# Transposing x out of DRAM instead of SBUF in a convolution kernel that runs on TensorE

## The chip, the cores and the metric

The kernel runs on one core of a Trainium2 chip. The metric is the device time in microseconds of one execution. The profile of one execution stands beside it; its span, from the first to the last instruction, is a little shorter than the time.

## The reference

A causal convolution over the sequence with eight taps, each tap a full 512 x 512 matrix:

```python
B, S, D, K = 8, 4096, 512, 8
out = np.zeros_like(x)                       # x: [B, S, D] float32
for k in range(K):                           # kernel: [K, D, D] float32
    shifted = x if k == 0 else np.concatenate(
        [np.zeros((B, k, D), np.float32), x[:, :-k, :]], axis=1)
    out += np.matmul(shifted, kernel[k])
```

## The kernel before

The 32768 rows of x are cut into 128 runs of 256 rows, one run for each partition. A step of the loop takes the next K = 8 rows of every run; there are NIT = 32 steps. TensorE needs x with its feature dimension on the partitions, so every step transposes its 8 x 128 rows of x, in two halves of four (h = 0, the low half, and h = 1, the high half), into the tile XT.

The way of x in the kernel before: GpSimd issues a DMA that reads 1 MB of f32 and writes it, cast to bf16, into an SBUF tile `xin` of 128 x 2048. SyncE then issues a DMA transpose from `xin` to a half of XT. The pool holds two `xin` buffers, so the load of a half waits until the transpose of the half two before it has read its buffer.

```python
xpool = ctx.enter_context(tc.tile_pool(name="x", bufs=2))
XT = spool.tile([P, K, D], bf, name="XT")
...
def load(out, src):
    nc.gpsimd.dma_start(out=out, in_=src)            # line 80 of the kernel

xin = {}

def load_x(i, h):
    xin[i, h] = xpool.tile([P, 4, D], bf, name="xin")
    load(xin[i, h], xr[:, K * i + 4 * h:K * i + 4 * h + 4, :])

def transpose_x(i, h):                               # line 89
    nc.sync.dma_start_transpose(
        out=XT[:, 4 * h:4 * h + 4, :].rearrange("p j (c m) -> p (j c) m", m=P),
        in_=xin[i, h].rearrange("p j d -> p (j d)"))
```

The eight taps are not multiplied one by one. The kernel uses a nested scheme of sums and differences (three levels, each of which needs three products in place of four), so VectorE forms sums of rows of XT (D1, D2, D4, D21, D42 and so on) and sums of results in PSUM. In a step there are three nodes, MID, LO and HI, with nine products of four matmuls each. The sums that read a freshly transposed half first are:

```python
def prep_m():                                        # reads XT[0:2], of the low half
    tt(D1[:, 0:2], XT[:, 7::-7], XT[:, 0:2], ADD)
    tt(pairs(D2[:, 1:5]), pairs(XT)[:, 3::-3], pairs(XT)[:, 0:2], ADD)

def prep_d4(h):
    a, b = (XT[:, 4:8], XT[:, 0:4]) if h == LO else (XT[:, 0:4], XT[:, 4:8])
    tt(D4[:, 4 * h:4 * h + 4], a, b, ADD)            # h == HI needs the new high half
```

The steady loop, one pass for each node. All engines run their own instructions in the order in which they are written here:

```python
for k, (i, a) in enumerate(order):                   # a: MID, LO, HI for each step i
    ...
    if a == MID and more:
        transpose_x(i + 1, 0)
    node_l(cur, 0, LO)
    node_l(cur, 0, HI)
    if nxt:
        node_a0(nxt)
        node_u(nxt)
    node_l(cur, 1, LO)
    node_e(cur, 0)                                   # result out of PSUM, or stored
    if nxt:
        node_seed(nxt, 0)
        node_seed(nxt, 1)
        node_dts(nxt)
    if a == MID:
        prep_d421(LO)
        prep_d41(HI)
    elif a == LO:
        if more:
            prep_m()
        prep_d421(HI)
    elif more:
        prep_d41(LO)
        prep_d42(LO)
        prep_d21()
    if nxt:
        for b_ in range(2):
            node_v(nxt, b_)
            node_d(nxt, b_)                          # VectorE: dts and v to the seed of node_l
    if a == MID:
        prep_d42(HI)
        prep_d27()
    elif more:
        prep_d4(LO if a == LO else HI)
    node_l(cur, 1, HI)
    if k + 2 < len(order):
        node_a1(k + 2)
    node_e(cur, 1)
    if a == LO and more:
        transpose_x(i + 1, 1)
        if i + 2 < NIT:
            load_x(i + 2, 0)
            load_x(i + 2, 1)
```

Steps 0 and 1 stand ahead of the loop in an order of their own, in which the loads and transposes appear so (all other work cut):

```python
load_x(0, 0); load_w(4); ...; load_x(0, 1); load_x(1, 0); ...; load_w(1); load_x(1, 1)
load_x(2, 0); load_x(2, 1); mid_acc(HI, LO)          # an accumulating DMA on a weight, SBUF to SBUF
transpose_x(1, 1); ...; transpose_x(2, 0); ...; load_x(3, 0); ...
load_x(3, 1); ...; transpose_x(2, 1); ...
```

The halves (0, 0), (0, 1) and (1, 0) are transposed on TensorE at the start; the other 61 are DMA transposes.

Of the kernel before, what the change touches and what calls it, by code (L numbers as in the profile page):

```python
# [22 lines left out]
def kernel(  # L23
# [7 lines left out]
    B, S, D = x.shape  # L31
    K = kernel.shape[0]
    P = 128
# [5 lines left out]
    bf = mybir.dt.bfloat16  # L39
# [12 lines left out]
    xpool = ctx.enter_context(tc.tile_pool(name="x", bufs=2))  # L52
# [26 lines left out]
    def load(out, src):  # L79
        nc.gpsimd.dma_start(out=out, in_=src)  # L80

    xin = {}

    def load_x(i, h):
        xin[i, h] = xpool.tile([P, 4, D], bf, name="xin")
        load(xin[i, h], xr[:, K * i + 4 * h:K * i + 4 * h + 4, :])

    def transpose_x(i, h):
# [52 lines left out]
    H, HF = XT, D421.bitcast(f32).rearrange("p (t b) d -> p t (b d)", b=2)  # L141
    nc.sync.dma_start(out=HF, in_=xr[:, RUN - 4:RUN, :])
    load_x(0, 0)
    zero = spool.tile([P, D], bf, name="zero")
    nc.vector.memset(zero, 0.0)  # L145
# [218 lines left out]
    transpose_pe("he", 1, H, 1, 4)  # L364
    load_w(7)
    load_x(0, 1)
    nc.vector.tensor_copy(out=XF[:, 6:8], in_=bank["xb"])
    tt(D2, XF[:, 1:6], XF[:, 3:8], ADD)
    fill(pair(2))
    tt(D4[:, 2:4], XF[:, 2:4], XF[:, 6:8], ADD)  # L370
    load_x(1, 0)
    direct(0, 2)
    tt(to(E4[:, 1:4]), prev(bank["he"]), to(XF[:, 1:4]), ADD)
# [278 lines left out]
```

## Time and profile before

| | |
|---|---|
| time, median of 2 runs | 779.34 us (779.1 to 779.57) |
| span of the profiled execution | 777.3 us |
| TensorE (PE) busy | 766.8 us, 99% |
| VectorE (DVE) busy | 657.5 us, 85% |
| ScalarE (ACT) busy | 284.9 us, 37% |
| granted TensorE clock | 1.000 |
| HBM read, written | 77.33 MB, 67.11 MB |
| DMA transposes | 61, median 6.1 us from issue to landing |
| loads of x | 64, median 5.9 us from issue to landing |

Busy time says how long an engine had something running; a matmul is pipelined, so a busy TensorE need not be one at its peak. In the lines of a timeline the columns are: start in us, duration in us, engine, line of the kernel, operation, output <- input by the program's names, their shapes, how many instructions are merged (x1), and in brackets the idle time of the engine ahead of it with what ended it. PE is TensorE, SPq the instruction queue of SyncE, POOL GpSimd. A transpose's or store's duration on SPq is the time for which it holds SyncE's queue, not the time until its data has landed. The queue lines of the page give packets, megabytes and the time that the packets took as a share of sixteen DMA engines over the span.

### The profile page before, as it was taken

Reading aid. Unit: us, or ns where it says so; the run is one execution under the profiler, and the core shown is the slowest. Engines: PE = TensorE matmul, PEld = TensorE weight load, DVE = VectorE, ACT = ScalarE, POOL = GpSimd, SP = SyncE. Lnnn points to the kernel's source line nnn. Section 1 sums busy time; section 2 is a strip of 40 time slices with the busy share of each in tenths; the row PEclk is TensorE's granted clock in tenths of the full one; section 3 lists DMA queues with packets and bytes.
Section 4 is the critical chain, followed back from the end, with each engine's and each line's share of the span. In section 5 each row is a group of like instructions: output and inputs, shape, how many; then the busy total and the mean of one; then the engine's idle time right before and its main releaser. Section 6 shows DMA issues by size and latency. Waiting matters only on the chain.

```text
span 777.3 us, 9450 instructions
## 1 busy us (share of the span) xinstructions
PE 766.8 (99%) x3584; PEld 347.3 (45%) x3584; DVE 657.5 (85%) x766; ACT 284.9 (37%) x462; POOL 42.3 (5%) x80
## 2 busy tenths in 40 slices
PE   7999999999999999999999999999999999999997
PEld 3444444444444444444444444444444444444443
DVE  4999988898888898888898888898888898888895
ACT  3553343333343333343333343333343333343332
POOL 4000000000000000000000000000000000000000
PEclk9999999999999999999999999999999999999999
DMA  9986878868786877787877878877697867687843
GB/s 199 211 125 170 226 185 178 208 159 190 164 199 163 197 172 189 164 198 169 194 171 187 164 174 190 207 162 188 163 187 176 207 158 190 165 186 179 204 133 121
DMA packets 159373, 139.42 MB, mean 179 GB/s; under 512 B 130144, under 2 KB 134240, under 8 KB 159200
## 3 DMA queue, kind: packets, MB, share of 16 engines
q1 hardware_dynamic: 145456, 99.89, 46.1%
q0 software_dynamic: 13728, 38.67, 31.6%
q8 instruction: 28, 0.46, 0.2%
q10 hardware_dynamic: 144, 0.26, 0.1%
q14 instruction: 17, 0.14, 0.1%
HBM read 77.33 MB, written 67.11 MB: 186 GB/s over the span
## 4 chain that ended last, share of the span: by engine, by line
PE 96%; DMA 2%; POOL 1%; ACT 0%; issue 0%; DVE 0%; DVEq 0%; POOLq 0%
PE pp L197 96%; DMA xin<-in_x_dram 2%; POOL w L80 0%; PE pp L186 0%; ACT y L295 0%; DVE y L76 0%; DVE pp L76 0%; POOL xin L80 0%; DVEq L647 0%; ACT pp L256 0%; ACT pp L244 0%; POOL XT L80 0%; PE pp L180 0%; POOL ident masks.py:199 0%; POOL ident masks.py:197 0%
## 5 line engine op out<-in xcount | busy, mean ns | idle before, releaser
L197 PE MATMUL pp<-w,D 128*128 128x512 bf16 x3280 | 715.5, 379 | 1.3 <-DVE w L76 0.9
L197 PEld LDWEIGHTS <-D 128*128 128x128 bf16 x3280 | 320.4, 98 | 389.8 <-issue 2.8
L76 DVE TENSOR_TENSOR D<-D 128x1024 bf16<-128x1024 bf16 (+1 forms) x252 | 228.2, 945 | 1.6 <-ACT D L353 1.6
L76 DVE TENSOR_TENSOR y<-pp,ms 128x1024 f32<-128x1024 f32 (+1 forms) x121 | 146.5, 1212 | 45.5 <-PE pp L197 45.4
L76 DVE TENSOR_TENSOR D<-XT 128x2048 bf16<-128x2048 bf16 (+2 forms) x153 | 142.1, 946 | 8.5 <-DMA XT<-xin 6.7
L244 ACT COPY pp<-pp 128x512 f32<-128x512 f32 x95 | 54.1, 570 | 256.0 <-PE pp L197 256.0
L256 ACT COPY pp<-pp 128x512 f32<-128x512 f32 x95 | 54.1, 570 | 170.6 <-PE pp L197 167.6
L76 DVE TENSOR_TENSOR pp<-dts,pp 128x512 f32<-128x512 f32 x95 | 65.5, 690 | 46.2 <-ACT dts L262 44.6
L299 ACT COPY ms<-pp 128x1024 f32<-128x1024 f32 x60 | 61.0, 1016 | 33.1 <-PE pp L197 33.1
L80 POOL DMA_DIRECT2D xin<-in_x_dram x64 | 34.2, 535 | 688.3 <-DMA XT<-xin 670.6
L272 DVE SCALAR_TENSOR_TENSOR pp<-pp,dts 128x512 f32<-128x512 f32 x95 | 65.9, 693 | 3.2
L262 ACT COPY dts<-pp 128x512 f32<-128x512 f32 x95 | 57.4, 604 | 2.0 <-PE pp L197 2.0
L258 ACT ACTIVATE pp<-pp 128x512 f32<-128x512 f32 x95 | 56.0, 589 | 1.2 <-DVE y L76 1.2
L197 PE MATMUL pp<-w,XT 128*128 128x512 bf16 x120 | 30.8, 379 | 0.0
L76 DVE TENSOR_TENSOR w<-w,w 128x2048 bf16<-128x2048 bf16 x18 | 21.6, 1219 | 0.4 <-DMA w<-in_kernel_dram 0.2
L197 PEld LDWEIGHTS <-XT 128*128 128x128 bf16 x120 | 11.7, 98 | 14.2
L180 PE MATMUL pp<-zero 128*128 128x512 bf16 x24 | 8.9, 505 | 2.4 <-DVE zero L145 1.2
L197 PE MATMUL pp<-w,w 128*128 128x512 bf16 x36 | 9.0, 379 | 1.3 <-ACT pp L244 0.7
L197 PE MATMUL pp<-w,F 128*128 128x512 bf16 x36 | 8.9, 379 | 0.0
L338 DVE MEMSET D<- 128x64 bf16 x2 | 0.2, 112 | 8.2 <-ACT D L351 7.7
L80 POOL DMA_DIRECT2D w<-in_kernel_dram x8 | 6.0, 766 | 0.8 <-DMA w<-in_kernel_dram 0.8
L197 PEld LDWEIGHTS <-w 128*128 128x128 bf16 x36 | 3.5, 97 | 5.8 <-issue 2.1
(55 smaller groups left out, 70.6 us busy)
## 6 DMA issues: line engine op xcount, KB each, us to landing
out_dram<-y SPq DMA_DIRECT2D x123, 512.0 KB, 3.5
xin<-in_x_dram POOLq DMA_DIRECT2D x64, 512.0 KB, 5.9
w<-in_kernel_dram POOLq DMA_DIRECT2D x8, 512.0 KB, 15.9
D<-in_x_dram SPq DMA_DIRECT2D x1, 1024.0 KB, 4.9
out_dram<-ms SPq DMA_DIRECT2D x2, 512.0 KB, 4.2
out_dram<-f SPq DMA_DIRECT2D x2, 512.0 KB, 3.7
XT<-xin SPq DMA_TRANSPOSE x61, 6.1
w<-w POOLq DMA_DIRECT2D x1, 512.0 KB, 9.9
```

The source lines that it names most:

```text
L76: nc.vector.tensor_tensor(out=o, in0=a, in1=b, op=op)
L80: nc.gpsimd.dma_start(out=out, in_=src)
L180: nc.tensor.matmul(pw[:, h], lhsT=zero[:, 0:P], rhs=zero, start=True, stop=True)
L197: nc.tensor.matmul(bank, lhsT=comp[:, c * P:(c + 1) * P], rhs=w[:, c, :], start=start and c == 0, stop=c == DC - 1, skip_group_check=True)
L244: nc.scalar.copy(out=n.q[:, 0], in_=n.q[:, 1])
L256: nc.scalar.copy(out=n.p[b_][:, 1], in_=n.q[:, 1])
L258: nc.scalar.mul(out=n.p[b_][:, 1], in_=n.q[:, 1], mul=-1.0)
L262: nc.scalar.copy(out=n.dts, in_=n.q[:, 0])
L272: nc.vector.scalar_tensor_tensor(out=p[:, 0], in0=p[:, 1], scalar=-1.0, in1=n.dts, op0=MUL, op1=SUB)
L299: nc.scalar.copy(out=ms[b_], in_=p)
L338: nc.vector.memset(z[:, :, 0:D:G], 0.0)
```

## The change

From the fourth step on (i = 3, counted from 0) the cast load of x writes into one of six DRAM buffers instead of one of two SBUF buffers, and the DMA transpose reads its source there. Steps 0 to 2 keep the SBUF tiles. What is computed stays the same, and so do the order of the instructions on each engine and the destination of the transposes. The aim is to take the staging copy of x out of SBUF and to give the loads more buffers to run ahead into.

```diff
@@ -81,8 +81,11 @@
 
     xin = {}
 
+    dpool = ctx.enter_context(tc.tile_pool(name="xd", bufs=6, space=bass.MemoryType.DRAM))
+
     def load_x(i, h):
-        xin[i, h] = xpool.tile([P, 4, D], bf, name="xin")
+        pool = xpool if i < 3 else dpool
+        xin[i, h] = pool.tile([P, 4, D], bf, name="xin" if i < 3 else "xd")
         load(xin[i, h], xr[:, K * i + 4 * h:K * i + 4 * h + 4, :])
 
     def transpose_x(i, h):
```

## The prediction

> **What bounds the kernel now.** I read the page's chain of work that ended last first, then the merged instructions of one steady period, then what one pair of transposes took to land, then the DMA queues. The chain, in order of time, ends so:
>
> ```profile
> 45.87 726.95 PE pp L197 x3364
> 772.82 0.02 issue
> 772.85 0.69 DVE y L76
> ```
>
> From 45.87 us on TensorE never waits. 726.95 us / 3364 matmuls = 216.1 ns each, and the starts of nearly all matmuls in the trace are 215 or 216 ns apart, whatever the DMAs do beside them. Nothing that the change touches lies on this stretch, so it can only leave it alone or put waits into it. Before 45.87 us the change alters nothing, as the first affected load comes later. That leaves next to nothing to win.
>
> The stretch holds 3364 / 108 = 31 periods (a step of the loop is three nodes of nine products of four matmuls: 108 x 216.1 ns = 23.3 us). Each period needs one transpose for each half of x. The merged timeline of one period, the lines that matter:
>
> ```profile
> 171.48 0.53 POOL L80 DMA_DIRECT2D xin<-in_x_dram  x1 [12.18 <-DMA XT<-xin]
> 173.93 4.82 SPq L89 DMA_TRANSPOSE XT<-xin  x1
> 176.90 0.69 DVE L76 TENSOR_TENSOR pp<-dts,pp 128x512 f32<-128x512 f32 x1 [1.69 <-ACT dts L262]
> 179.49 0.57 ACT L244 COPY pp<-pp 128x512 f32<-128x512 f32 x1 [2.80 <-PE pp L197]
> 182.30 1.82 DVE L76 TENSOR_TENSOR D<-XT 128x1024 bf16<-128x1024 bf16 x2
> 185.17 0.69 DVE L76 TENSOR_TENSOR pp<-dts,pp 128x512 f32<-128x512 f32 x1
> 187.27 0.57 ACT L244 COPY pp<-pp 128x512 f32<-128x512 f32 x1 [2.75 <-PE pp L197]
> 189.21 3.24 SPq L89 DMA_TRANSPOSE XT<-xin  x1
> 194.27 1.23 DVE L76 TENSOR_TENSOR D<-XT 128x2048 bf16<-128x2048 bf16 x1
> 194.71 0.53 POOL L80 DMA_DIRECT2D xin<-in_x_dram  x1 [13.19 <-DMA XT<-xin]
> ```
>
> The low half is issued at 173.93 and first read at 182.30 (prep_m); the high half is issued at 189.21 and first read at 194.27 (prep_d4). Landing of these two, low half first, as the trace gives it for the transpose line in windows around each:
>
> ```profile
> DMA to landing us min/median/max: 6.5/6.5/6.5
> ```
>
> ```profile
> DMA to landing us min/median/max: 5.0/5.0/5.0
> ```
>
> So the low half lands at 180.4, 1.9 us ahead of its reader, and the high half at 194.2, only 0.1 us ahead. What VectorE does after a late read decides whether TensorE feels it. TensorE needs node_d's first half at the start of the next node, which I take from the copy that follows node_a1, the last product of a node: 179.4, 187.2. In the MID node that node_d ended at 176.90 + 0.69 = 177.6 after an idle 1.69 us, so between the high half's read and TensorE there are 0.1 + 1.7 + 1.8 = 3.6 us of room. In the LO node it ended at 185.9, so the low half has 1.9 + 1.3 = 3.2 us. **The transposes may land at about issue + 8.6 (high) and issue + 9.7 (low) before TensorE waits.**
>
> The page's queues give the other limit:
>
> ```profile
> q1 hardware_dynamic: 145456, 99.89, 46.1%
> q0 software_dynamic: 13728, 38.67, 31.6%
> ```
>
> Together 78% of sixteen DMA engines: 0.78 x 23.3 = 18.1 us of each period, and 5.2 us free.
>
> **What the Trainium skill says.** The Trainium skill, page "DMA: Bandwidth & Descriptors", section "Latency and other measured facts", gives a transpose 261 GB/s with a non-contiguous middle dimension: 524 KB then take an estimated 2.0 us on the engines. The trace is a little slower, with SBUF as source: the packet records of the high half run from issue + 1.91 to + 4.51 us, 2.6 us or 202 GB/s.
> The same page of the Trainium skill, section "Why small descriptors are slow (HBM only)", puts the penalty on small pieces of HBM and exempts SBUF to SBUF. That is the risk here: a transpose has 2048 packets of 256 bytes. No run so far shows such pieces read from HBM.
> The same page of the Trainium skill, section "Queues, rings and completion order", says that an engine takes turns between queues at packet granularity. The trace agrees badly: beside the load issued at 171.48, the store issued at 173.43 and the transpose begin their packets only at about 176 and 177.2, when the load's are done. A short transfer waits for loads already queued.
>
> **The change part by part.** It removes no instruction of TensorE, VectorE or ScalarE, and no load and no transpose. It moves 58 of the 61 transposes and 58 of the 64 loads (29 of 32 steps, two halves) to DRAM buffers.
>
> Loads: each still reads 1 MB of f32. Its packets (8 KB read, 4 KB written, per engine 8) take 322 ns in the median, about the 25 GB/s at which the source is read; a store's 4 KB packet into DRAM takes 159. The read side still sets the pace, so I add nothing. A later receipt from DRAM costs nothing: six buffers instead of two put a load three steps ahead of its use.
>
> Traffic: 58 x 0.524 = 30.4 MB more written to HBM and as much read, 144 to 205 MB, 264 GB/s over the span. That alone is no reason to wait.
>
> Transposes: the cost that decides. From SBUF a packet takes 22.7 ns in the mean; 128 packets per engine are 2.9 us. For HBM as source I draw a line through the two kinds of cast loads: 2048 bytes read in 98 ns (weights), 8192 in 322 (x). Slope 224 / 6144 = 0.0365 ns per byte, intercept 23.3 ns. At 256 bytes: 23.3 + 9.3 = 33 ns, 128 x 33 = 4.2 us, against the 2.6 measured: each transpose lands 1.6 us later, at about issue + 6.6 and + 8.1. Both are inside the room. DMA occupancy rises by 2 x (4.2 - 2.9) = 2.6 us to 20.7 of 23.3 us, 89%. In the steady state the sum is 0 us on the path. VectorE will idle before prep_d4 more often, and catch up.
>
> Start: with two buffers, the load of step 3 waited for the transpose of step 2 (it issued at 58.09 us). With six free DRAM buffers GpSimd has nothing to wait for, and issues all six loads of steps 3, 4 and 5 right after the accumulate at 44.94, from 45.8 to about 49 us. Each is 8 x 0.4 = 3.3 us of all engines, so some 20 us of queue. The transpose of step 2's low half issues at 46.19, lands at 57.5 now and is read at 61.46, 4 us of room plus about 2 to TensorE. If it shares evenly with the burst it ends some 3 us later: no loss. If it queues behind the loads already issued (two or three), 7 to 10 us later: 1 to 4 us lost once. I put +1.5 us.
>
> Sum: 779.3 + 0 + 1.5 = 780.8 us.
>
> **The rivals.**
> First, the read from HBM is slow enough to become the bound. At 48 ns per packet a transpose takes 6.1 us and the high half's room is used up; at about 43 ns (5.5 us) the engines' 5.2 free us per period are gone. At 60 ns, 7.7 us each, a period holds 12.3 + 15.4 = 27.7 us of DMA, and the 29 affected periods cost 29 x 4.4 = 128 us. For it: the small pieces, latency under load, and a kernel whose high half has 0.1 us to spare already. Against it: the estimate has a third in hand, and the skill's transpose figure is fast. One case in four.
> Second, the burst is worse than I think, and store and transpose queue behind all six loads: the low half of step 2 lands near 74, 12 us late, TensorE loses 6 to 10 us, about 1%.
> Third, the transposes get faster: SBUF no longer carries source and load, and SyncE is held for less than the 3.2 to 4.8 us of now. But a transpose that lands early helps nobody: TensorE waits for nothing. It would end between 777 and 780 us.
>
> **The range and the chances.** Below is closed by the fixed pitch of 216 ns: 2% off would be 15.6 us, more than all TensorE idles in the whole run (777.3 - 766.8 = 10.5). So faster gets 0.01. The likely case lies from 778 to 784; the worse burst reaches 790; slow HBM reads, with a weight of 0.24, run from 800 far upwards. An interval for 8 in 10 is 777.5 to 810; 781 as the point.
>
> **What would show it.** Right: the chain again one piece of TensorE of about 727 us; transposes from DRAM landing 6 to 8.5 us after issue, 256-byte packets at 25 to 40 ns; DMA share near 0.85 to 0.9; a knot of six loads at 46 us and a landing of step 2's low half after 58 us. Wrong: VectorE's idle before reads of XT (now 6.7 us, six times in the whole run) growing past 100 us, with TensorE waiting for node_d in every period; that would mean packets over 45 ns. A transpose that lands sooner than from SBUF would refute the straight line, though not the time.

## The result, and the profile after

| | before | after |
|---|---|---|
| time, median of 2 runs | 779.34 us | 900.64 us |
| span of the profiled execution | 777.3 us | 898.7 us |
| TensorE busy | 766.8 us, 99% | 771.2 us, 86% |
| mean granted TensorE clock | 1.000 | 0.935 |
| HBM written | 67.11 MB | 97.52 MB |
| loads of x to landing, median | 5.9 us | 21.2 us (those into DRAM) |
| DMA transposes to landing, median | 6.1 us | 5.4 us (from DRAM), most 60.2 us |

The ratio is 1.156, 95% interval 1.152 to 1.159: 121 us slower, far outside the predicted range of 777.5 to 810.

The page of the changed kernel, with the span in 40 slices (22.5 us each; digits are tenths busy, PEclk tenths of the full TensorE clock):

```profile
PE   7980813106999999999999999999999999999997
...
PEclk9995865656999999999999999999999999999999
DMA  9999999999554444444455544454545444445553
```

All of the loss lies in slices 3 to 10. After some 217 us TensorE is as busy as before, and the DMA engines are *less* busy than before (0.49 in the windows from 216.7 to 869.7 us, where the kernel before has 0.73 to 0.81): work that belongs there has been done earlier. The instructions of GpSimd at the start of that stretch show which:

```profile
44.53 0.53 POOL L80 DMA_DIRECT2D xin<-in_x_dram  x1 [15.74 <-DMA XT<-xin]
45.06 0.90 POOL L172 DMA_DIRECT2D w<-w  x1
45.62 3.47 POOL L80 DMA_DIRECT2D xd<-in_x_dram  x6
52.08 0.52 POOL L80 DMA_DIRECT2D xd<-in_x_dram  x1 [2.99 <-DMA xin<-in_x_dram]
54.70 0.52 POOL L80 DMA_DIRECT2D xd<-in_x_dram  x1 [2.10 <-DMA w<-w]
57.40 0.52 POOL L80 DMA_DIRECT2D xd<-in_x_dram  x1 [2.18 <-DMA xd<-in_x_dram]
```

The six loads go out, as expected, but then a seventh follows, and an eighth, each when an earlier *load or accumulate* has landed, eight DMAs back (the built program gives GpSimd's DMAs eight semaphores in turn). None waits for a transpose to free a buffer. The last of the 58 loads is issued at 197.9 us and the last load packet ends at 217.7 us. GpSimd's waits over the whole run (us in total, times, longest) say the same, first in the kernel before, then in the changed one:

```profile
POOL xin L80 <- DMA XT<-xin: 670.6, 59, 15.6
```

```profile
POOL xd L80 <- DMA xd<-in_x_dram: 117.5, 50, 3.3
```

The six buffers don't exist. In the built program each of the 58 `dpool.tile(...)` calls has an address of its own, while the `xin` tiles of the SBUF pool share two: with this way of allocation the pool's count of six doesn't bind in DRAM, and with it fell the only thing that held the loads back.

What became of the transposes beside this flood of loads: first the landing of step 2's low half (issued at 46.1), from the transpose line in a window around it, then that of the 55 transposes from 220 us on:

```profile
DMA to landing us min/median/max: 44.9/44.9/44.9
```

```profile
DMA to landing us min/median/max: 5.0/5.4/7.5
```

The next two, step 2's high half (issued at 97.6) and step 3's low half (147.6), took

```profile
DMA to landing us min/median/max: 48.6/48.6/48.6
```

```profile
DMA to landing us min/median/max: 60.2/60.2/60.2
```

All that follow the flood land about as soon as in the kernel before. VectorE's waits for transposes, first before and then after (the first two of the three have their source in SBUF):

```profile
DVE D L76 <- DMA XT<-xin: 6.7, 6, 1.8
```

```profile
DVE D L76 <- DMA XT<-xd: 70.3, 30, 48.7
DVE D L76 <- DMA XT<-xin: 64.2, 2, 34.8
```

TensorE's timeline has one hole for each of the three, and VectorE ends all of them:

```profile
93.56 1.87 PE L200 MATMUL pp<-w,F 128*128 128x512 bf16 x4 [28.40 <-DVE pp L275]
...
149.39 0.61 PE L200 MATMUL pp<-w,D 128*128 128x512 bf16 x1 [33.97 <-DVE D L76]
...
208.55 1.89 PE L200 MATMUL pp<-w,D 128*128 128x512 bf16 x4 [46.88 <-DVE D L76]
```

28.4 + 34.0 + 46.9 = 109 us of the 121. The first line also shows where most of the rest goes: its four matmuls take 1.87 us (they start 379 to 427 ns apart instead of 216), because the clock was halved in the hole and comes back only some 3 us after the hole's end, at 96.9 us. Counted over the run, matmuls at half clock cost 7 us. The Trainium skill describes this ("TensorE: Matmul & The Clock Gate", "Part 1: The HAM clock gate"): an idle TensorE falls to half rate. The trace agrees: PEclk reads 5 to 8 (0.5 to 0.8) in the slices with holes and 9 (at least 0.9) outside. So the low clock is a result of the holes, not their cause.

### The profile page after: what moved, and what is told of

It reads as the page before. It is cut to its first block, busy times and chain, and to the rows that moved or that the text cites. A ratio compares the mean times of both kernels' runs of the same rounds, so it can differ in the third digit from the quotient of the medians.

```text
span 898.7 us, 9321 instructions
## 1 busy us (share of the span) xinstructions
PE 771.2 (86%) x3513; PEld 349.1 (39%) x3584; DVE 658.0 (73%) x766; ACT 285.0 (32%) x462; POOL 41.4 (5%) x80
## 3 DMA queue, kind: packets, MB, share of 16 engines
HBM read 77.33 MB, written 97.52 MB: 195 GB/s over the span
## 4 chain that ended last, share of the span: by engine, by line
PE 75%; DMA 12%; another core or an unknown queue 5%; DVE 4%; SPq 2%; issue 1%; POOL 0%; ACT 0%; DVEq 0%; ACTq 0%; POOLq 0%
PE pp L200 74%; DMA XT<-xin 5%; DMA out_dram<-y 4%; DMA xin<-in_x_dram 2%; DVE D L76 2%; DMA XT<-xd 2%; DVE y L76 1%; SPq L92 1%; SPq L285 1%; DVE pp L76 0%; DVE pp L275 0%; POOL w L80 0%; ACT pp L259 0%; PE pp L189 0%
## 5 line engine op out<-in xcount | busy, mean ns | idle before, releaser
L80 POOL DMA_DIRECT2D xd<-in_x_dram x58 | 30.3, 552 | 122.5 <-DMA xd<-in_x_dram 117.5
L200 PE MATMUL pp<-w,F 128*128 128x512 bf16 x34 | 9.8, 413 | 28.5 <-DVE pp L275 28.4
L200 PEld LDWEIGHTS <-F 128*128 128x128 bf16 x36 | 3.8, 104 | 33.5 <-issue 30.0
## 6 DMA issues: line engine op xcount, KB each, us to landing
xd<-in_x_dram POOLq DMA_DIRECT2D x58, 512.0 KB, 21.2
xin<-in_x_dram POOLq DMA_DIRECT2D x6, 512.0 KB, 13.6
```

What stands on the lines that cost most here:

```text
L200: nc.tensor.matmul(bank, lhsT=comp[:, c * P:(c + 1) * P], rhs=w[:, c, :], start=start and c == 0, stop=c == DC - 1, skip_group_check=True)
```

## The experiments

**Theory Flood.** The loads run ahead without waiting for any transpose; while they queue, transposes are starved; DRAM as the source of a transpose costs nothing. **Rival Source.** Reading 256-byte pieces of DRAM, or the added DRAM traffic, costs, as the prediction feared. **Rival start-up.** Something peculiar to the first 200 us.

### A real ring of DRAM buffers, of 2, 6 and 16

The tiles are made once and used in turn, so that a load must wait for the transpose that last read its tile (n is 2, 6 or 16):

```diff
-    dpool = ctx.enter_context(tc.tile_pool(name="xd", bufs=6, space=bass.MemoryType.DRAM))
+    dpool = ctx.enter_context(tc.tile_pool(name="xd", bufs=1, space=bass.MemoryType.DRAM))
+    ring = [dpool.tile([P, 4, D], bf, name=f"xd{m}") for m in range(n)]
...
-        pool = xpool if i < 3 else dpool
-        xin[i, h] = pool.tile([P, 4, D], bf, name="xin" if i < 3 else "xd")
+        if i < 3:
+            xin[i, h] = xpool.tile([P, 4, D], bf, name="xin")
+        else:
+            xin[i, h] = ring[(2 * (i - 3) + h) % n]
```

> Two DRAM tiles made once and used in turn, so a load waits for the transpose two halves before it, as with the two SBUF buffers of the kernel before; the transposes still read DRAM. Theory Flood (the 58 loads run ahead because each DRAM tile has memory of its own, and they starve transposes and stores): no flood, so 779.3 us, between 778.5 and 780.5; transposes land about 5.4 us after issue. Rival Source (reading small pieces of DRAM, or the added DRAM traffic, is itself what costs): 860 to 900 us.

> Six DRAM tiles used in turn, what the count of six in the change seems to ask for. Flood: a burst of six loads at 46 us; when the first packets of step 2's low transpose start, some 40 load packets per engine are still queued, and one 256-byte packet goes per load packet (0.31 us): 40 x 0.31 + 88 x 0.02 = 14 us, landing near 66 us instead of 57.5; TensorE loses about 2.5 us: 782 us, between 780 and 785. Source: 860 to 900 us.

> Sixteen DRAM tiles used in turn. Flood: 16 loads are 128 load packets per engine, as many as the transpose of step 2's low half has, so this one lands as late as in the changed kernel (near 90 us) and every later one on time: a loss of about 28 us, 807 us, between 802 and 813. Source: 860 to 900 us. A theory in which only the depth of prefetch as such matters, and not the number of load packets beside a transpose, would put ring6 and ring16 close together.

| kernel | time | ratio to before, 95% interval | step 2's low half lands after | hole in TensorE |
|---|---|---|---|---|
| ring of 2 | 780.02 us | 1.0007 (0.9999 to 1.0015) | 14.1 us | none |
| ring of 6 | 789.44 us | 1.013 (1.011 to 1.015) | 24.1 us | 7.8 us |
| ring of 16 | 809.83 us | 1.039 (1.037 to 1.040) | 44.7 us | 28.4 us |
| as changed (58 tiles) | 900.64 us | 1.156 (1.152 to 1.159) | 44.9 us, and two more | 28.4, 34.0, 46.9 us |

The ring of 2 has all 58 loads into DRAM and all 58 transposes out of it, and runs in the time of the kernel before: Source falls. Its transposes land 6.3 us after issue (median of 55), not the 5.4 that I expected; before it was 6.1. GpSimd's waits in the ring of 2 name transposes again:

```profile
POOL xd L80 <- DMA XT<-xd: 657.2, 56, 41.0
```

The ring of 16 came out as worked out, 810 for 807. Here too no more than eight DMAs of GpSimd were under way at a time (ten waits name the DMA eight back), as in the changed kernel: what more buffers lengthen is the time for which the queue stays full. It has this one hole:

```profile
93.34 1.86 PE L203 MATMUL pp<-w,F 128*128 128x512 bf16 x4 [28.38 <-DVE pp L278]
```

The ring of 6 missed its 780 to 785. TensorE's timeline around its hole:

```profile
63.95 1.03 PE L203 MATMUL pp<-w,zero 128*128 128x512 bf16 x4
72.73 1.86 PE L203 MATMUL pp<-w,F 128*128 128x512 bf16 x4 [7.76 <-DVE pp L278]
```

The sign and the single hole are right, the size is not. I had 40 load packets ahead of the transpose at 0.31 us. But the load of step 2's high half and the accumulate came first and had only just gone through when the transpose's first packet went at 51.1 us, so all 48 packets of the six loads were still queued, and the interleaved stretch took 17.3 us, 0.36 us for each. It landed at 70.2 and not 66; 7.8 us of hole and seven matmuls at half clock (1.4 us) are most of the 10.1 us.

### Half of the flood, in the middle of the run

```diff
-        pool = xpool if i < 3 else dpool
-        xin[i, h] = pool.tile([P, 4, D], bf, name="xin" if i < 3 else "xd")
+        pool = xpool if i < 17 else dpool
+        xin[i, h] = pool.tile([P, 4, D], bf, name="xin" if i < 17 else "xd")
```

> As the changed kernel, but SBUF is used up to step 16 and the unbounded DRAM tiles from step 17: 30 loads instead of 58 run ahead, near 375 us. Flood: 30 loads are 80 us of the engines instead of 154; a loss in proportion, about 60 us: 840 us, between 825 and 855, with a hole in TensorE near 380 to 470 us and none at 50 to 210. If the loss belonged to the start of the kernel alone (ramp, accumulating DMA, first steps), it would vanish: 779 to 785.

848.81 us, ratio 1.089 (1.087 to 1.090). TensorE's two holes:

```profile
432.72 1.89 PE L200 MATMUL pp<-w,D 128*128 128x512 bf16 x4 [36.19 <-DVE D L76]
...
475.91 0.59 PE L200 MATMUL pp<-w,D 128*128 128x512 bf16 x1 [26.49 <-ACT pp L259]
```

30 loads cost 69.5 us, 2.3 us each; 58 cost 121.3, 2.1 each. The start-up isn't needed for the loss. Both starved transposes here are those of step 16 and have their source in SBUF (as had two of the three in the changed kernel, those of step 2), which speaks against Source once more.

### The same flood in smaller packets

A load into DRAM is cut into two of two rows (split in two) or four of one row (split in four); the bytes stay. Load packets then read 4 KB or 2 KB instead of 8 KB.

```diff
-        load(xin[i, h], xr[:, K * i + 4 * h:K * i + 4 * h + 4, :])
+        if i < 3:
+            load(xin[i, h], xr[:, K * i + 4 * h:K * i + 4 * h + 4, :])
+        else:
+            for r in (0, 2):
+                load(xin[i, h][:, r:r + 2, :], xr[:, K * i + 4 * h + r:K * i + 4 * h + r + 2, :])
```

> The changed kernel, with every load into DRAM cut into two of two rows each, so that a load packet reads 4 KB instead of 8 KB; bytes, buffers and run-ahead as before. Theory Turns (one 256-byte transpose packet goes per load packet, so a starved transpose lasts 128 load packets): a load packet takes about 0.17 us (4 KB on the line through the measured 98 and 322 ns), 128 of them 22 us: the transpose of step 2's low half lands about 27 us after issue instead of 44, its hole in TensorE is about 11 us instead of 28.8. More transposes then fall into the flood, which is as long as before: 870 us, between 850 and 890. Rival Bytes (transpose and loads share the engines by bytes or by time): that transpose still lands 40 to 49 us after issue, time near 900.

> As split2, with four loads of one row each: a load packet reads 2 KB, 98 ns as the weights show. Turns: 128 x 0.1 = 13 us, so step 2's low half lands about 18 us after issue, with a hole of 3 us or less; about 185 us of flood now cover some eight to ten transposes of 10 us hole each: 860 us, between 830 and 885. Bytes: landing 40 to 49 us, time near 900 or above.

| kernel | load packet, median | step 2's low half: its packets run | lands after | its hole | time (ratio) |
|---|---|---|---|---|---|
| as changed | 322 ns | 38.7 us | 44.9 us | 28.4 us | 900.64 us (1.156) |
| split in two | 172 ns | 21.9 us | 27.9 us | 11.6 us | 897.92 us (1.152, 1.151 to 1.154) |
| split in four | 98 ns | 13.6 us | 20.4 us | 4.0 us | 914.49 and 920.71 us (1.174 and 1.181) |

Two further runs of the kernel split in four took 929.92 and 931.28 us, over 1.5% more than its fastest; the table has the two others.

For this transpose Turns holds: 38.7, 21.9 and 13.6 us are 128 times 0.30, 0.17 and 0.11 us, about one load packet for each 256-byte transpose packet. The packet records show it directly: beside its 128 packets per engine, 116, 115 and 117 load packets per engine start (counts per engine are all packets over 16), and some 15 of the loads' 4-byte packets. Bytes falls; it had the landing unchanged. The whole time is a miss in both: I had expected 870 and 860. Six transposes instead of three fell into the flood of the kernel split in two, with holes of 11.6, 15.0, 26.0, 22.5, 16.9 and 12.9 us, 105 in sum, and a flood that lasted to 243 us instead of 218. In the one split in four the flood lasted to 350 us, with holes of up to 13.5 us.

Why the sum stays nearly the same when split in two, as far as I can argue it: 58 loads are 464 packets per engine, and a transpose passes up to 128 of them, so some three and a half fit, or twice as many of half the length in smaller packets. The total then is the time of the queue of loads, not of one transpose. This fits the counts of the unsplit kernels (one hole at 16 loads, two at 30, three at 58), but the sizes of the later holes in the split kernels I can't derive. In the one split in four only 60 to 72 load packets per engine start beside each of the next three transposes, so that Turns alone doesn't explain those, and what part of split four's excess is matmuls at half clock (27 us in the profiled run) and what the longer flood is not taken apart.

### Without the early stores

The second and third transpose took longer from issue than the first. SyncE issues the stores too, so they might be the ones starved.

```diff
     def store(i, a, b_, y):
+        if i < 3:
+            return
```

This leaves out 12 stores of two rows of every run each, the results of steps 0 to 2 (24 rows, which the expectation below calls tiles).

> The changed kernel without the stores of steps 0, 1 and 2: the first 24 result tiles aren't written, nothing else is left out. If transposes alone starve TensorE: three holes again, of about 29, 29 and 29 us instead of 28.8, 34.6 and 47.5, because the second and third transpose no longer stand behind stores in SyncE's queue; 876 us, between 862 and 890. If it is the stores that hold SyncE and the result buffers: the second and third hole go away, 800 to 830.

One run: 887.51 us, with these holes:

```profile
93.56 1.86 PE L200 MATMUL pp<-w,F 128*128 128x512 bf16 x4 [28.20 <-DVE pp L275]
144.25 9.43 PE L200 MATMUL pp<-w,D 128*128 128x512 bf16 x36 [27.75 <-DVE D L76]
186.11 1.89 PE L200 MATMUL pp<-w,D 128*128 128x512 bf16 x4 [32.43 <-DVE D L76]
...
211.38 4.00 PE L200 MATMUL pp<-w,D 128*128 128x512 bf16 x9 [8.85 <-ACT pp L259]
```

The first three holes become more alike, as the packets of each of the three now begin within 5 us of its issue and span 38 to 39 us, and the fraction of a fourth transpose that the remaining load packets still catch adds 8.9 us. So transposes alone starve TensorE; the stores lengthen the second and third hole by 6 and 14 us, and 13 us of the loss is all that leaving them out gives back.

An SBUF ring deeper than two, to ask whether loads into SBUF would flood as loads into DRAM do, wasn't tried: not even one tile more fits beside the other pools. No run beat the kernel before, and none was to be expected to: TensorE has no hole to fill after 45.9 us.

## Why the prediction was wrong, step by step

**The bound and the closed side: right.** The pitch of 216 ns held in every kernel here, outside the stretches at half clock, and nothing came out faster.

**"With six free DRAM buffers GpSimd ... issues all six loads": the step that failed.** The number was 58. I took the pool's count from the diff as a fact of the program; in SBUF the profile shows it (GpSimd waits for transposes), in DRAM nothing had shown it yet. From there "+1.5 us" followed instead of +121. A second step failed beside it, "if it shares evenly with the burst it ends some 3 us later: no loss": with six loads and no more, the ring of six, step 2's low half landed 12.7 us later than before, and the loss was 10.1 us.

**The second rival looked at the right place, with another mechanism.** It had store and transpose queue behind all six loads, the transpose landing near 74 us, for 6 to 10 us. A true ring of six landed at 70.2 us and cost 10.1 us. But the transpose did not queue behind the loads: its first packet went at 51.1 us and the rest took turns with theirs. With 48 load packets against its 128 both mechanisms let it end soon after the burst, so the near agreement is partly luck. They part at 58 loads: queued behind all of them, the transpose would have landed after 217.7 us; it landed at 91. The main line took the milder of two guesses about sharing.

**"The trace agrees badly" with the Trainium skill: a wrong reading.** I had seen one load of eight packets per engine, with a transpose behind it that began only when it was done, and concluded that short transfers wait for all that is queued. Even there the store had begun at 175.9 us, before the load's last packet ended at 176.8; why the transpose began only 3.2 us after its issue stays open. In the flood the skill's "DMA: Bandwidth & Descriptors", "Queues, rings and completion order", is borne out: queues take turns, and a turn is one packet. What hurts is that a transpose's turn carries 256 bytes and a load's reads 8 KB: 31 ns (median beside the flood; 18 alone) against 322. Taking turns is cheap for a store of eight packets per engine (the one issued at 94.7 us, with no transpose ahead of it, landed after 8.4 us; before, 2.6), and ruinous for a transpose of 128.

**"33 ns" for a packet read from DRAM: wrong, harmless.** The mean packet of a transpose takes 20 ns from DRAM after the flood (median over the transposes; 21 in the ring of 2), and 22 ns from SBUF in the kernel before; from about 106 us on they landed 4.9 to 9.2 us after issue in the ring of 2, 4.9 to 8.3 before. The straight line through the two cast loads doesn't carry over to a transpose: its median packet takes 18 ns from either memory. What the skill says of small pieces of HBM against SBUF ("DMA: Bandwidth & Descriptors", "Why small descriptors are slow (HBM only)") isn't borne out for this transfer. Nor did "a later receipt from DRAM" show: loads into DRAM landed in 5.7 us (median, ring of 2), into SBUF in 5.9.

**Steady state "0 us on the path": right.** From 216.7 to 403.2 us there are 862 weight loads, eight periods of 108, in 186.5 us, 23.3 each, and VectorE waited 18.8 us in 27 of the 55 transposes after 220 us, more than the 6.7 of before, and caught up, as foretold. The ring of 2 shows it for the whole run: 1.0007. The delay behind it was smaller than the 1.6 us worked out: in the ring of 2 the high half landed 5.2 us after issue in the median, against 5.0 before, and the low half 7.0 against 6.5. With 0.1 us to spare at the high half, that is enough for VectorE to wait.

**DMA occupancy "to 89%": wrong.** It stayed at 0.78 in the ring of 2, as the packets did not get slower.

**The first rival (slow reads of DRAM)** had held all the weight that I gave to times above 800 us. The result lay there for another reason.

## What to carry to other kernels

A buffer count is also a brake: a change of memory space, pool or allocation that removes the wait of a load for its buffer removes the pacing of the whole queue, so look in the built program (or at what the issuing engine waits for) whether the buffers are really reused. Keep transfers of many small packets, such as these DMA transposes, away from a long queue of large packets: here they got about one turn for each large packet. Where TensorE has no idle time, running further ahead with loads can't win anything and is only a risk; keep the depth at what hides the latency.

## What the runs showed of the hardware that I had not expected

- A DMA transpose of 128 x 2048 bf16 is 2048 packets of 256 bytes, 128 for each of 16 engines. Beside a standing queue of loads it took 38.7, 21.9 and 13.6 us for load packets of 322, 172 and 98 ns; alone 2.6 us.
- A transpose of this shape reads DRAM as fast as SBUF: 20 to 22 ns a packet from either (median over the transposes of their mean packet).
- HBM read on the page is 77.33 MB in the kernel before, the changed kernel and the ring of 2 alike, though the last two read 30.4 MB of staging buffers again; written went up by just 30.4 MB. The page's figure for reads does not seem to count the sources of transposes, and I would not build on it.
- After a hole of 7.8 us seven matmuls still ran at half clock, 1.4 us in all.
